# Moving the large GpSimd tensor operations of the layer ends to VectorE in a two-layer encoder

## The chip, the cores and the metric

The kernel runs on one core of a Trainium2 chip. The metric is the device time in microseconds (us) of one execution; the median of several executions is used. One execution was recorded by the hardware profiler, and all rows below are of that one. Five engines of the core run side by side, each with its own queue of instructions in a fixed order: TensorE (PE in the rows, its weight loads PEld), VectorE (DVE), ScalarE (ACT), GpSimd (POOL) and SyncE (SP, which here only starts DMA transfers).

## The reference

Two encoder layers on 512 tokens of width 1024. Each layer has a mixer (an mLSTM branch and a dilated attention branch) and a SwiGLU channel mixer of width 2816. Each of the two sub-layers ends in a scaled residual and a LayerNorm:

```
h = layer_norm(x)
for l in range(DEPTH):
    ...
    u = h * (1.0 + sc1) + sh1
    y = mixer(u, ...)
    h = layer_norm(DN_ALPHA * h + g1 * y, ln1_g[l], ln1_b[l])
    u = h * (1.0 + sc2) + sh2
    y = swiglu(u, w1[l], w3[l], w2[l])
    h = layer_norm(DN_ALPHA * h + g2 * y, ln2_g[l], ln2_b[l])
```

The shift, scale and gate vectors (sh, sc, g) are products of the conditioning vector with `w_ada`, plus a bias. All values are 32-bit floats.

## The kernel before

**Products.** Each float matrix product is done as three matmuls: both factors are split into a high part (a cast on ScalarE, line 87) and a low part (source minus high, a tensor_tensor on one engine, line 88), and high x high, high x low and low x high are summed (lines 91 to 93). The low part of nearly every weight tile is made on VectorE. `split` takes the engine as an argument; before the change GpSimd gets it for the early weights named below.

**Layer ends.** `out_norm` (line 408) is the end of a sub-layer. It is called four times; its name stands ahead of every tile: `o0` and `o1` are the mixer ends of layers 0 and 1, `f0` and `f1` the ends of the channel mixers. It multiplies the sub-layer's activations by the last weight (1024 output columns as two halves, y0 and y1; four blocks of 128 tokens, t = 0 to 3), adds the gated result to the residual (`gate`, `add`, lines 444 and 447), takes statistics (450, 352, 354; the power -1/2 is a tiny operation on GpSimd, line 355) and normalises (365). `to_u` then transposes the normalised block on TensorE (`turn`, line 381), applies the next scale and shift on ScalarE (`high`, lines 389 and 391) and makes the low part on VectorE (`low`, line 395).

**What is kept between sub-layers.** The kernel stores the normalised rows without LayerNorm's own g and b. The next layer end loads them (`loads`, line 426, tiles `f0x`, `o1x`, `f1x`) and applies g and b there: lines 430 and 431, one multiplication and one addition of 128x1024 for each token block, on GpSimd. That is done for four blocks in f0 and f1 and for two in o1; the other two blocks of o1 get it already in f0's `store` (lines 488 and 489), ahead of the store itself, which GpSimd's queue starts.

**Early weights.** While the last half of a layer end is running, the weights of the next product are made ready: `ahead` in the mixer ends splits the first two tiles of `w1` and `w3` (tiles `zw`; 2 layers x 4 tiles x 2 halves = 16 operations of 128x512 on line 88), and `ahead_next` in f0 splits the first query weights of layer 1 (`fw<-aqraw`, 8 operations of 128x512).

**Order.** Most of the program is put in order by the framework's scheduler, which places an instruction by the time it expects it to be ready: so the loads of f0 and f1 (lines 426 to 431) run far ahead, inside the channel mixer (`z` products of `w1` and `w3`, `sl` the activation, `L1337` the product with z3, `fl` its low part). The channel mixer's loop also carries background work: the `w_ada` products (`acc`, lines 281 and 283, one 128x512 operation for each of eight loaded tiles `aw`) and a transposition of the sum on TensorE (`adaps`, line 293). The second half of each layer end is written out by hand (`manual_schedule`): its order is the order of the code. In f0 and f1 TensorE goes through the last half in steps of two weight tiles (`pairs`) for blocks 2 and 3, and the steps of blocks 0 and 1 are dealt out between them by the tables `SD` and `SF`; the last six tiles are then done block by block (`columns`).

Of the kernel before, what the change touches and what calls it, by code (L numbers as in the profile page):

```python
# [14 lines left out]
ALU = mybir.AluOpType  # L15
# [5 lines left out]
KT = 8  # L21
# [44 lines left out]
def encoder(ctx: ExitStack, tc: tile.TileContext, a, depth):  # L66
    nc = tc.nc
    alpha = 4 ** 0.25
    V, S, G, Y = nc.vector, nc.scalar, nc.gpsimd, nc.sync
# [13 lines left out]
    def raw_tile(name):  # L83
        return wpool.tile([P, 2048], F32, tag="raw", name=name, bufs=RAW)

    def split(hi, lo, src, eng=None):
        S.copy(hi, src)  # L87
        (eng or V).tensor_tensor(lo, src, hi.bitcast(F32), op=ALU.subtract)  # L88
# [24 lines left out]
    def w_pair(name, off, k, n):  # L113

        return [wpool.tile([P, 1024 + WPAD], F32R, tag=t, name=name + t[1])[:, off:off + k * n]
                .rearrange("p (k n) -> p k n", n=n) for t in ("wh", "wl")]

    def w_feature(src, ktiles, name, own=None, count=2, eng=None):


        n = src.shape[1]
        cols = 2048 // ktiles
        srcv = src.rearrange("(k p) n -> p k n", p=P)
        for c0 in range(0, n, cols):
            cw = min(cols, n - c0)
            raw = raw_tile(name)
            rv = raw[:, :ktiles * cw].rearrange("p (k n) -> p k n", k=ktiles)
            Y.dma_start(rv, srcv[:, :, c0:c0 + cw])
            for j in range(cw // P):
                r = rv[:, :, j * P:(j + 1) * P]  # L130
                if own is not None and c0 // P + j < count:
                    yield split_own(r, ktiles, own, eng)
                    continue
                wh, wl = w_pair(name, 0, ktiles, P)
                split(wh, wl, r, G if name in POOL else V)
                yield [wh[:, k, :] for k in range(ktiles)], [wl[:, k, :] for k in range(ktiles)]

    def split_own(r, ktiles, own, eng):

        out = [], []  # L140
        for k in range(0, ktiles, 4):
            wh, wl = own(), own()
            split(wh[:], wl[:], r[:, k:k + 4, :], eng)
            for o, w in zip(out, (wh, wl)):
                o.extend(w[:, i, :] for i in range(4))
        return out

    def w_token(src, c0, cw, ktiles, name, own=None, own_k=(), early=False):

        srcv = src.rearrange("(k p) n -> p k n", p=P)  # L150
        per_raw = 2048 // cw
        per = 1024 // cw
        cuts = list(range(0, ktiles, per_raw)) + [ktiles]
        raws = []

        def load():
            i = len(raws)
            if i + 1 < len(cuts):
                k0, k1 = cuts[i], cuts[i + 1]
                raw = raw_tile(name)  # L160
                raws.append(raw[:, :(k1 - k0) * cw].rearrange("p (k n) -> p k n", n=cw))
                Y.dma_start(raws[i], srcv[:, k0:k1, c0:c0 + cw])

        if early:
            load()
        for i, (k0, k1) in enumerate(zip(cuts, cuts[1:])):
            load()
            rv = raws[i]
            for j in range(0, k1 - k0, per):
                m = min(per, k1 - k0 - j)  # L170
                if k0 + j in own_k:
                    for h in range(m):
                        wh, wl = own(), own()
                        split(wh[:], wl[:], rv[:, j + h, :])
                        yield wh[:], wl[:]
                else:
                    wh, wl = w_pair(name, SH if cw == 256 else 0, per, cw)
                    split(wh[:, :m], wl[:, :m], rv[:, j:j + m, :])
                    for h in range(m):
                        yield wh[:, h, :], wl[:, h, :]  # L180
# [227 lines left out]
    def out_norm(act, ktiles, w, l, which, prev, todo, own, final, aff, u, hin, hout, keep, name, ahead, after, fslot=None):  # L408

        with ExitStack() as st:  # L410
            lp = pool(st, name + "L", side="right")
            xs = [lp.tile([P, D], F32, name=f"{name}x{t}") for t in range(NT)]
            rows = {}

            def row(key, src, q=Y):
                rows[key] = lp.tile([P, D], F32, tag="row" + key, name=name + key)
                q.dma_start(rows[key][:], src.partition_broadcast(P))

            def loads():
                row("g", adarow[l][which][0])  # L420
                if prev is not None:
                    row("s", prev[0])
                    row("b", prev[1])
                for t in range(NT):
                    x = xs[t]
                    Y.dma_start(x[:], hin[t * P:(t + 1) * P, :])
                    if prev is None:
                        V.tensor_scalar(x[:], x[:], mu0[t][:, 0:1], mu0[t][:, 3:4], op0=ALU.subtract, op1=ALU.mult)
                    elif t in todo:
                        G.tensor_tensor(x[:], x[:], rows["s"][:], op=ALU.mult)  # L430
                        G.tensor_tensor(x[:], x[:], rows["b"][:], op=ALU.add)
                if own is not None:
                    row("s", own[0], G)
                    row("b", own[1], G)
# [50 lines left out]

            def store(t):
                if own is not None and t < 2:
                    G.tensor_tensor(xs[t][:], xs[t][:], rows["s"][:], op=ALU.mult)
                    G.tensor_tensor(xs[t][:], xs[t][:], rows["b"][:], op=ALU.add)
                (G if own is not None and t < 2 else S).dma_start(hout[t * P:(t + 1) * P, :], xs[t][:])  # L490

            def side_steps(y01):

                todo = []
                for t in range(2):
                    steps = consume_steps(y01[t], t, 1) + norm_steps(t)
                    if not final:
                        turn, high, low = to_u(lp, xs[t], t, aff, u, name + "n")
                        steps.extend([turn, step(high, 0), step(low, 0), step(high, 1), step(low, 1), step(store, t)])
                    todo.extend(zip((SF if final else SD)[t], steps))  # L500
                if not final:
                    for i, ats in enumerate((AQL, AQS)):
                        todo.extend((at, step(ahead, i, n)) for n, at in enumerate(ats))
                return todo
# [16 lines left out]
            if keep:  # L521
# [6 lines left out]
                w1 = w_token(w, T, T, ktiles, name + "v", oh, range(4, ktiles), True)  # L528
                for k in range(4):
                    wk_ = next(w0)  # L530
                    for t in range(NT):
                        part(acc[t], t, k, *wk_)
                    if k == 1:
                        loads()
# [13 lines left out]
            else:  # L548
                for k, wk_ in enumerate(w_token(w, 0, T, ktiles, name + "w")):
                    for t in range(NT):  # L550
                        part(acc[t], t, k, *wk_)
                    if k == 1:
                        loads()
# [19 lines left out]
                w1 = w_token(w, T, T, ktiles - 2, name + "v", fslot, range(2 * heads, ktiles - 6))  # L573
# [70 lines left out]
    with ExitStack() as st:  # L644
        lp = pool(st, "L0", side="right")
        xs = [lp.tile([P, D], F32, name=f"x0{t}") for t in range(NT)]
# [74 lines left out]
        with tc.manual_schedule(engines=ENG):  # L721
            for f in range(KT):
                wh, wl, _ = wq
# [11 lines left out]
    for l in range(depth):  # L735
# [554 lines left out]
        def hgw():  # L1290
            return PW.tile([P, 4, P], F32R, tag="hgw", name="zw", bufs=16)

        w1 = w_feature(a["w1"][l], KT, "w1", hgw, 2, G)
        w3 = w_feature(a["w3"][l], KT, "w3", hgw, 2, G)
        quad, zs, third = [], [], []

        def ahead():
# [22 lines left out]
        for i in range(FT):  # L1320
# [12 lines left out]
            t = F.tile([P, T], F32, tag="sl", name="sl", bufs=1)  # L1333
# [14 lines left out]
        first_w, first, first_k, aq_raw = [], [], {}, []  # L1348

        def fslot():  # L1350
            return F.tile([P, T], F32R, tag="f", name="fw", bufs=2 * FT)

        def ahead_next(part, n):

            if part == 0:
                c0 = COL_A + 512 * (n // 2)
                raw = F.tile([P, T], F32, tag="f", name="aqraw", bufs=2 * FT)[:].rearrange("p (k n) -> p k n", k=4)
                Y.dma_start(raw, a["w_in"][l + 1][512 * (n % 2):512 * (n % 2) + 512, c0:c0 + P]
                            .rearrange("(k p) n -> p k n", p=P))
                aq_raw.append(raw)  # L1360
            else:
                wh, wl = (fslot()[:].rearrange("p (k n) -> p k n", k=4) for _ in range(2))
                split(wh, wl, aq_raw[n], G)
                if n % 2 == 0:
                    first_w.append(([], []))
                for o, w in zip(first_w[-1], (wh, wl)):
                    o.extend(w[:, i, :] for i in range(4))
# [61 lines left out]
```

## Time and profile before

| | us |
|---|---|
| median of 3 runs | 2280.37 (2280.28 to 2283.35) |
| profiled execution, its own time | 2288.52 |
| span of the profiled execution | 2286.7 |
| TensorE busy | 2201.6 (96%) |
| VectorE busy | 1315.9 (58%) |
| ScalarE busy | 884.0 (39%) |
| GpSimd busy | 321.6 (14%) |
| mean granted TensorE clock | 0.985 |

The span is the time from the first to the last instruction of the profiled execution; its own time is 1.8 us longer, and 8.15 us above the median of the runs without a profile. Busy times are of all instructions of an engine, and overlap between engines. The granted clock is the share of TensorE's full speed (2.4 GHz) that the chip allowed; 0.5 is 1.2 GHz.

### The profile page before, as it was taken

Reading aid. Unit: us, or ns where it says so; the run is one execution under the profiler, and the core shown is the slowest. Engines: PE = TensorE matmul, PEld = TensorE weight load, DVE = VectorE, ACT = ScalarE, POOL = GpSimd, SP = SyncE. Lnnn points to the kernel's source line nnn. Section 1 sums busy time; section 2 is a strip of 40 time slices with the busy share of each in tenths; the row PEclk is TensorE's granted clock in tenths of the full one; section 3 lists DMA queues with packets and bytes.
Section 4 is the critical chain, followed back from the end, with each engine's and each line's share of the span. In section 5 each row is a group of like instructions: output and inputs, shape, how many; then the busy total and the mean of one; then the engine's idle time right before and its main releaser. Section 6 shows DMA issues by size and latency. Waiting matters only on the chain.

```text
span 2286.7 us, 30972 instructions
## 1 busy us (share of the span) xinstructions
PE 2201.6 (96%) x12353; PEld 1836.4 (80%) x12353; DVE 1315.9 (58%) x2242; ACT 884.0 (39%) x1465; POOL 321.6 (14%) x318
## 2 busy tenths in 40 slices
PE   6999999999999999999989999999999999999998
PEld 5878877878888878788878788788888879788886
DVE  8655458778554766564654544577764454633346
ACT  3544345544333522222354443455543324223222
POOL 4100013222000240000040000233300022200001
PEclk8999999999999999999999999999999999999999
DMA  8523322232343466554543223112212344423334
GB/s 239 186 83 107 101 66 97 74 111 80 111 157 113 155 206 205 189 193 167 189 152 98 61 92 107 56 62 69 74 56 92 111 157 157 152 83 102 100 112 157
DMA packets 244064, 278.79 MB, mean 122 GB/s; under 512 B 10280, under 2 KB 191184, under 8 KB 243920
## 3 DMA queue, kind: packets, MB, share of 16 engines
q1 hardware_dynamic: 238848, 258.97, 35.1%
q0 software_dynamic: 3584, 12.58, 1.6%
q10 hardware_dynamic: 1488, 5.26, 0.6%
q8 instruction: 97, 1.59, 0.3%
q14 instruction: 47, 0.39, 0.1%
HBM read 264.18 MB, written 12.60 MB: 121 GB/s over the span
## 4 chain that ended last, share of the span: by engine, by line
PE 75%; DVE 14%; ACT 3%; issue 3%; DMA 3%; POOL 2%; POOLq 0%; DVEq 0%; ACTq 0%; SPq 0%
PE z L93 6%; PE z L92 6%; PE z L91 6%; DVE cy L1081 4%; DMA aw<-in_w_ada 2%; PE aq L91 2%; PE ak L91 2%; PE f1y L92 2%; PE av L91 2%; PE f1y L91 2%; PE f1y L93 2%; PE av L93 2%; PE av L92 2%; PE aq L93 2%; PE aq L92 2%
## 5 line engine op out<-in xcount | busy, mean ns | idle before, releaser
L283 DVE SCALAR_TENSOR_TENSOR acc<-aw,cact,acc 128x512 f32<-128x512 f32 x140 | 118.3, 845 | 49.8 <-DMA aw<-in_w_ada 47.6
L1081 DVE SCALAR_TENSOR_TENSOR cy<-zp,vcols,cy 128x512 f32<-128x512 f32 x128 | 115.6, 903 | 10.4 <-ACT cy L1079 8.5
L87 ACT CAST w3h<-w 128x1024 fp32r<-128x1024 f32 x40 | 42.1, 1053 | 157.3 <-PE z L92 153.2
L88 POOL TENSOR_TENSOR wqkl<-wqk,wqkh 128x1024 fp32r<-128x1024 f32 x32 | 78.0, 2438 | 161.4 <-ACT wqkh L87 159.5
L978 ACT ACTIVATE xs<-xs,sm 128x512 f32<-128x512 f32 x64 | 46.2, 723 | 133.3 <-DVE sm L977 129.6
L87 ACT CAST w1h<-w 128x1024 fp32r<-128x1024 f32 x40 | 42.0, 1050 | 139.9 <-PE z L92 134.9
L88 DVE TENSOR_TENSOR w1l<-w,w1h 128x1024 fp32r<-128x1024 f32 x40 | 49.4, 1234 | 77.3 <-ACT w1h L87 77.3
L1337 DVE TENSOR_TENSOR sl<-sl,z 128x512 f32<-128x512 f32 x44 | 30.2, 687 | 104.9 <-PE z L93 101.2
L976 DVE CUSTOM_DVE_ANT_0 xs<-sc,bias 128x512 f32<-128x512 f32 x64 | 43.9, 691 | 74.7 <-PE sc L970 63.7
L91 PE MATMUL z<-um0h,w3h 128*128 128x512 f32 x160 | 64.2, 401 | 4.0 <-DVE sl L1337 4.0
L91 PE MATMUL z<-um1h,w3h 128*128 128x512 f32 x160 | 63.5, 397 | 1.8 <-DVE sl L1337 1.8
L93 PE MATMUL z<-um1h,w3l 128*128 128x512 f32 x160 | 63.6, 398 | 1.0 <-DVE w3l L88 1.0
L93 PE MATMUL z<-um0h,w3l 128*128 128x512 f32 x160 | 63.9, 400 | 0.5 <-DVE w3l L88 0.5
L92 PE MATMUL z<-um0l,w3h 128*128 128x512 f32 x160 | 63.8, 399 | 0.0
L92 PE MATMUL z<-um1l,w3h 128*128 128x512 f32 x160 | 63.2, 395 | 0.0
L91 PE MATMUL z<-um0h,w1h 128*128 128x512 f32 x160 | 63.1, 394 | 0.0
L93 PE MATMUL z<-um0h,w1l 128*128 128x512 f32 x160 | 62.7, 392 | 0.0
L92 PE MATMUL z<-um0l,w1h 128*128 128x512 f32 x160 | 62.5, 391 | 0.0
L91 PE MATMUL z<-um1h,w1h 128*128 128x512 f32 x160 | 62.4, 390 | 0.0
L93 PE MATMUL z<-um1h,w1l 128*128 128x512 f32 x160 | 62.3, 390 | 0.0
L92 PE MATMUL z<-um1l,w1h 128*128 128x512 f32 x160 | 62.2, 389 | 0.0
L935 POOL DMA_DIRECT2D vrow<-nat x16 | 11.8, 736 | 345.0 <-ACT nat L928 344.9
(544 smaller groups left out, 7268.0 us busy)
## 6 DMA issues: line engine op xcount, KB each, us to landing
w<-in_w SPq DMA_DIRECT2D x44, 1024.0 KB
aw<-in_w_ada SPq DMA_DIRECT2D x160, 256.0 KB
wqk<-in_w_in SPq DMA_DIRECT2D x16, 1024.0 KB
wav<-in_w_in SPq DMA_DIRECT2D x12, 1024.0 KB
wak<-in_w_in SPq DMA_DIRECT2D x20, 512.0 KB
f0v<-in_w SPq DMA_DIRECT2D x10, 1024.0 KB
f1v<-in_w SPq DMA_DIRECT2D x10, 1024.0 KB
waq<-in_w_in SPq DMA_DIRECT2D x18, 512.0 KB
```

The costliest lines, as they stand in the source:

```text
L87: S.copy(hi, src)
L88: (eng or V).tensor_tensor(lo, src, hi.bitcast(F32), op=ALU.subtract)
L91: mm(out, lh, rh, start=first, stop=False)
L92: mm(out, lh, rl, start=False, stop=False)
L93: mm(out, ll, rh, start=False, stop=last)
L283: V.scalar_tensor_tensor(acc[:], raws[k][:], c, acc[:], op0=ALU.mult, op1=ALU.add)
L935: G.dma_start(rows[i0 * P:(i0 + 2) * P, :].rearrange("(i p) c -> p i c", p=P), nat[:])
L976: V.tensor_tensor_reduce(x[:], sc[:], bias_tile(ti), 1.0, -3e38, ALU.add, ALU.max, sm[:, 0:1])
L978: S.activation(x[:], x[:], AF.Exp, bias=sm[:, 1:2], scale=ch, accum_out=sm[:, 2:3])
L1081: V.scalar_tensor_tensor(y[:], zp[:, j:j + T], vec["conv"](j, n), y[:], op0=ALU.mult, op1=ALU.add)
L1337: V.tensor_tensor(t[:], t[:], p3[:], op=ALU.mult)
```

## The change

Lines 430, 431, 488 and 489 and the low parts of the early weights (line 88 as called by way of lines 1293, 1294 and 1363) go from GpSimd to VectorE. Nothing else is edited; the two stores of line 490 stay in GpSimd's queue.

```diff
                     elif t in todo:
-                        G.tensor_tensor(x[:], x[:], rows["s"][:], op=ALU.mult)
-                        G.tensor_tensor(x[:], x[:], rows["b"][:], op=ALU.add)
+                        V.tensor_tensor(x[:], x[:], rows["s"][:], op=ALU.mult)
+                        V.tensor_tensor(x[:], x[:], rows["b"][:], op=ALU.add)
...
             def store(t):
                 if own is not None and t < 2:
-                    G.tensor_tensor(xs[t][:], xs[t][:], rows["s"][:], op=ALU.mult)
-                    G.tensor_tensor(xs[t][:], xs[t][:], rows["b"][:], op=ALU.add)
+                    V.tensor_tensor(xs[t][:], xs[t][:], rows["s"][:], op=ALU.mult)
+                    V.tensor_tensor(xs[t][:], xs[t][:], rows["b"][:], op=ALU.add)
...
-        w1 = w_feature(a["w1"][l], KT, "w1", hgw, 2, G)
-        w3 = w_feature(a["w3"][l], KT, "w3", hgw, 2, G)
+        w1 = w_feature(a["w1"][l], KT, "w1", hgw, 2)
+        w3 = w_feature(a["w3"][l], KT, "w3", hgw, 2)
...
-                split(wh, wl, aq_raw[n], G)
+                split(wh, wl, aq_raw[n])
```

VectorE's queue gets 36 more rows of the kind shown below (a row may stand for several equal instructions); the queues of TensorE and ScalarE keep their order. GpSimd keeps the powers, the memsets, its DMAs and the splits of the mixer.

On VectorE, in the channel mixer of layer 0 (the places of the loads of f0; the four numbers 9233 to 9236 are the four token blocks), the scheduler puts the eight operations between those of two steps of the mixer's loop:

```order
 L88 TENSOR_TENSOR w1l<-w_7426,w1h 128x1024
+L430 TENSOR_TENSOR f0x_9233<-f0x_9233,f0s 128x1024
+L431 TENSOR_TENSOR f0x_9233<-f0x_9233,f0b 128x1024
+L430 TENSOR_TENSOR f0x_9234<-f0x_9234,f0s 128x1024
 L1337 TENSOR_TENSOR sl<-sl,z_7524 128x512
+L431 TENSOR_TENSOR f0x_9234<-f0x_9234,f0b 128x1024
+L88 TENSOR_TENSOR fl<-sl,fh 128x512
 L88 TENSOR_TENSOR w3l<-w_7432,w3h 128x1024
-L88 TENSOR_TENSOR fl<-sl,fh 128x512
+L430 TENSOR_TENSOR f0x_9235<-f0x_9235,f0s 128x1024
+L430 TENSOR_TENSOR f0x_9236<-f0x_9236,f0s 128x1024
+L431 TENSOR_TENSOR f0x_9235<-f0x_9235,f0b 128x1024
```

Seven of the eight new operations now stand in VectorE's queue among `L1337`, `fl` and `w3l` of one step of the loop; the eighth (`L431` of block 3) follows nine rows later, just ahead of the next `L1337`.

On VectorE, in the part of f0 written by hand (`f0vl` is the low part of a pair of the last weight, `uf0l` that of a block's next input, `fw<-f0v` and the last two `f0vl` the tiles of the `columns`):

```order
 L395 TENSOR_TENSOR uf0l<-f0nut,uf0h 128x4x128
+L488 TENSOR_TENSOR f0x_9233<-f0x_9233,f0s 128x1024
+L489 TENSOR_TENSOR f0x_9233<-f0x_9233,f0b 128x1024
 L88 TENSOR_TENSOR f0vl<-f0v,f0vh 128x1024
 L395 TENSOR_TENSOR uf0l<-f0nut,uf0h 128x4x128
 L88 TENSOR_TENSOR f0vl<-f0v,f0vh 128x1024
 L395 TENSOR_TENSOR uf0l<-f0nut,uf0h 128x4x128
+L488 TENSOR_TENSOR f0x_9234<-f0x_9234,f0s 128x1024
+L489 TENSOR_TENSOR f0x_9234<-f0x_9234,f0b 128x1024
 L88 TENSOR_TENSOR fw<-f0v,fw 128x512 x2
+L88 TENSOR_TENSOR fw<-aqraw,fw 128x512 x2
 L88 TENSOR_TENSOR f0vl<-f0v,f0vh 128x1024 x2
```

The scale and shift of blocks 0 and 1 now stand ahead of low parts of weights that TensorE reads next, and so does the first pair of early weights.

On VectorE, in o1 (blocks 2 and 3 are `o1x_16344` and `o1x_16345`):

```order
 L444 TENSOR_TENSOR o1tmp<-o1y_16351,o1g 128x512
+L430 TENSOR_TENSOR o1x_16344<-o1x_16344,o1s 128x1024
 L447 SCALAR_TENSOR_TENSOR o1x_16343<-o1x_16343,o1tmp 128x512
+L431 TENSOR_TENSOR o1x_16344<-o1x_16344,o1b 128x1024
+L430 TENSOR_TENSOR o1x_16345<-o1x_16345,o1s 128x1024
 L450 BN_STATS o1st_16347<-o1x_16343 128x6
+L431 TENSOR_TENSOR o1x_16345<-o1x_16345,o1b 128x1024
 L444 TENSOR_TENSOR o1tmp<-o1y_16352,o1g 128x512
```

The four operations now stand between the gating of block 1 and that of block 2; further down, four `zw` operations stand between the statistics of block 3 (first half) and the gating of block 0 (second half).

## Rows read from the trace of the kernel before

**Rows 1.** The page's first part: busy time, share of the span, instructions
```profile
PE 2201.6 (96%) x12353; PEld 1836.4 (80%) x12353; DVE 1315.9 (58%) x2242; ACT 884.0 (39%) x1465; POOL 321.6 (14%) x318
```
**Rows 2.** Busy time by stretch; columns PE, PEld, DVE, ACT, POOL, PEclk, DMA, GB/s
```profile
755.00:785.00 30.00, 29.48 (x165) 25.32 (x164) 24.46 (x36) 16.80 (x39) 13.85 (x12) 1.00 0.45 156
830.00:845.00 15.00, 10.53 (x37) 7.72 (x35) 11.24 (x13) 2.59 (x4) 5.33 (x4) 0.77 0.58 190
1138.00:1157.00 19.00, 13.59 (x59) 10.41 (x59) 16.29 (x11) 9.31 (x19) 12.89 (x7) 0.91 0.75 241
1157.00:1182.00 25.00, 21.70 (x123) 18.10 (x122) 17.41 (x20) 15.07 (x31) 14.95 (x13) 1.00 0.27 89
1876.00:1891.00 15.00, 11.40 (x34) 7.63 (x34) 14.36 (x14) 3.13 (x6) 11.09 (x7) 0.77 0.28 90
1957.00:1971.00 14.00, 11.21 (x39) 8.39 (x38) 9.85 (x11) 2.69 (x4) 3.03 (x3) 0.76 0.51 156
940.00:953.00 13.00, 10.81 (x43) 8.54 (x42) 7.26 (x12) 3.21 (x4) 0.00 (x0) 0.87 0.53 182
```
**Rows 3.** Instructions grouped by line, GpSimd: count | busy us, mean ns | idle before
```profile
L88 POOL TENSOR_TENSOR fw<-aqraw,fw 128x512 fp32r<-128x512 f32 x8 | 12.8, 1626 | 9.6 <-ACT fw L87 9.6
...
L430 POOL TENSOR_TENSOR f0x<-f0x,f0s 128x1024 f32<-128x1024 f32 x4 | 11.2, 2800 | 29.3 <-DMA f0x<-hspill 29.3
```
**Rows 4.** Timeline of VectorE where GpSimd is idle: start, duration, instruction
```profile
790.52 1.23 DVE L88 TENSOR_TENSOR w1l<-w,w1h 128x1024 fp32r<-128x1024 f32 x1 [0.26 <-ACT w1h L87]
791.66 1.22 DVE L88 TENSOR_TENSOR w3l<-w,w3h 128x1024 fp32r<-128x1024 f32 x1
...
1856.93 2.49 DVE L88 TENSOR_TENSOR o1o<-o1w,o1o 128x512 fp32r<-128x512 f32 x4
```
**Rows 5.** Timelines of GpSimd, VectorE and TensorE at the loads of f0
```profile
811.56 2.40 POOL L430 TENSOR_TENSOR f0x<-f0x,f0s 128x1024 f32<-128x1024 f32 x1 [29.32 <-DMA f0x<-hspill]
...
822.80 2.35 DVE L296 TENSOR_TENSOR scc<-scc,vcols 128x4 f32<-128x4 f32 x1
...
834.78 0.67 DVE L1337 TENSOR_TENSOR sl<-sl,z 128x512 f32<-128x512 f32 x1
...
847.82 0.16 DVE L296 TENSOR_TENSOR shc<-shc,vcols 128x4 f32<-128x4 f32 x1
...
835.60 0.76 PE L91 MATMUL z<-um0h,w3h 128*128 128x512 f32 x1 [3.96 <-DVE sl L1337]
```
**Rows 6.** Timelines of ScalarE, VectorE and TensorE at the end of f0
```profile
1136.45 1.05 ACT L87 CAST f0vh<-f0v 128x1024 fp32r<-128x1024 f32 x1 [1.67 <-PE f0y L93]
1139.17 1.06 ACT L87 CAST f0vh<-f0v 128x1024 fp32r<-128x1024 f32 x1 [1.67 <-PE f0y L93]
...
1140.13 2.91 DVE L365 TENSOR_SCALAR f0x<-f0x,f0nmv,f0nrs 128x1024 f32<-128x1024 f32 x1 [0.45 <-POOL f0nrs L355]
1142.96 3.38 DVE L88 TENSOR_TENSOR f0vl<-f0v,f0vh 128x1024 fp32r<-128x1024 f32 x1
...
1143.10 1.09 PE L381 MATMUL f0ntp<-ident,f0x 128*128 128x128 f32 x8 [0.33 <-DVE f0x L365]
...
1180.50 1.09 PE L381 MATMUL f0ntp<-ident,f0x 128*128 128x128 f32 x8
```
**Rows 7.** Timelines of VectorE and TensorE in o1
```profile
1870.12 0.69 DVE L444 TENSOR_TENSOR o1tmp<-o1y,o1g 128x512 f32<-128x512 f32 x1 [0.57 <-PE o1y L93]
...
1878.58 7.20 DVE L88 TENSOR_TENSOR o1o<-o1v,o1o 128x512 fp32r<-128x512 f32 x4
...
1880.76 0.50 PE L92 MATMUL o1y<-o1o,mh 128*128 128x512 f32 x1 [2.30 <-DVE o1o L88]
...
1893.77 1.03 PE L381 MATMUL o1ntp<-ident,o1x 128*128 128x128 f32 x8
```
**Rows 8.** VectorE's timeline at the loads of f1; TensorE's waits from 1918 us on
```profile
1960.19 0.68 DVE L1337 TENSOR_TENSOR sl<-sl,z 128x512 f32<-128x512 f32 x1
...
PE z L91 <- DVE sl L1337: 1.8, 1, 1.8
```

## The prediction

> **What bounds the kernel now.** I read the page's busy times first: TensorE works 96% of the span, every other engine at most 58% [rows 1]. So a change on VectorE and GpSimd can pay only where TensorE stands still or runs at a lower clock. Next I read TensorE's waits and, around them, the stretches of the four layer ends [rows 2]. The time lost in a stretch is its length less the PE busy time, plus (1 - PEclk) times its length: 0.5 us in o0 (755 to 785), 4.5 + 3.45 = 7.9 at the loads of f0 (830 to 845), 5.4 + 1.7 + 3.3 = 10.4 at the end of f0 (1138 to 1182), 3.6 + 3.45 = 7.05 in o1 (1876 to 1891), 2.8 + 3.35 = 6.15 at the loads of f1 (1957 to 1971): 32.0 us in all. That is the most the change can give back in these places.
>
> Then I read the timelines there, to see what is late. TensorE always waits for VectorE (for `sl`, `f0vl`, `o1o`), and VectorE is late because its instructions grow while GpSimd works on large tiles. `L296`, 128x4, takes 2.35 us while line 430 or 431 runs, and 0.16 us later on [rows 5]; `f0vl` takes 3.38 us [rows 6] where its like takes 1.22 [rows 4]; four `o1o` take 7.20 us [rows 7] against 2.49 [rows 4]. The reader should see that such an instruction lasts about as long as what is left of a GpSimd operation of 2.4 to 2.8 us [rows 3, 5], plus its own time. VectorE is blocked there, not overloaded.
>
> The SBUF — State Buffer page of the Trainium skill (Who interferes with whom) says that the two engines share a port pair which one of them holds for its whole instruction; the long 128x4 operation of this trace agrees. By that rule alone, all 32.0 us would return; this is the full recovery below.
>
> **The change, step by step.** Removed from GpSimd: 24 operations of 128x1024 at about 2.8 us and 24 of 128x512 at about 1.6 [rows 3]. Added to VectorE: the same 48. The trace has no `L430` on VectorE; the nearest rows are subtractions with the same two SBUF inputs and shape, which follow each other after 1.14 us (790.52 to 791.66) and take 2.49 / 4 = 0.62 us at 128x512 [rows 4]. GpSimd's own 2.8 us is the upper bound, and 0.62 the lower (as if size cost nothing); I take 1.14, since engine, shape and operands are the same. Added: 24 x 1.14 + 24 x 0.62 = 42 us, against 2286.7 - 1315.9 us in which VectorE is idle. What counts is where they stand, so I re-timed each place: the new order of VectorE's queue, undisturbed durations, TensorE at 0.227 us per 512-column matmul (two ScalarE casts of neighbouring weight pairs, 12 matmuls apart, are 2.72 us apart [rows 6]).
>
> *o0.* Four `zw` (2.5 us) come ahead of block 0's gating, but the VectorE work around them is no longer blocked. Block 0 is normalised at 765.0, when TensorE is ready to transpose it. Gain 0.5 us.
>
> *Loads of f0.* VectorE reaches `L430` when the first block lands (811.56, the end of GpSimd's wait [rows 5]). Eight operations add 9.1 us up to the second `L1337`, with `w1l`, `w3l` and the `acc` work between them; I get `L1337` done at about 828.5 instead of 835.45. TensorE stood ready for it at 835.60 - 3.96 = 831.64 [rows 5]: 3 us to spare. The low parts of w1 and w3 then come about 0.7 us before they are read, and the background sum, paced by its loads, just in time. Of 7.9 I take 7.5.
>
> *End of f0.* From 1140.13 on [rows 6]: `L365` of block 1 ends at 1140.9, the next `f0vl` at 1142.0, so TensorE transposes block 1 at 1142.6, not 1143.10, and does not wait behind it. The store's two operations (2.3 us) then stand before the next low parts. They delay the `f0vl` of the pair after next to 1150.1, where TensorE wants it at 1149.1: a wait of 1.0. Block 1's pair delays `fw` and, with two early weights, the `f0vl` behind: waits of 0.7 and 1.5. Four early weights (2.5 us) delay block 3's gating, and its transposition by 0.5. Without waits TensorE has 0.85 (transposition) + 4 x 2.72 (pairs) + 2 x 4.08 (last six tiles of blocks 2 and 3) + 0.85 + 42 x 0.12 (256-column products) = 25.8 us from 1142.6 to the transposition of block 3, which would be at 1168.4; now it is at 1180.50 [rows 6]. With the 3.8 us of new waits it comes at 1172.2. Gain 8.3 us.
>
> The Perfetto Trace Analysis page (Optimizing Scalar/DVE Operations) of the Trainium skill advises giving work to GpSimd when VectorE is saturated, and adds that this might not help because of the shared port. It speaks against the change, and is the third rival below.
>
> *o1.* After the gating at 1870.12 [rows 7] VectorE has two blocks to scale and shift (4.6 us) and then the usual steps, and starts the four `o1o` at 1878.5, as now (1878.58), but ends them at 1881.0, not 1885.8. TensorE, ready for the first at 1880.76 - 2.30 = 1878.46, waits 0.8. After that four `zw` (2.5 us) stand in front of block 0's gating, and its normalised rows come at 1889.5. TensorE would transpose them at 1887.15 (1878.1 + 2.72 for the rest of block 0 + 5.44 for block 1 + 0.9), so it waits 2.35 us, on a wait that does not exist now. The transposition is at 1889.5 instead of 1893.77 [rows 7]: 4.2 us. In the stretch 940 to 953 TensorE stood for about 2.2 us and the granted clock was 0.87, which cost 0.13 x 13 = 1.7 us [rows 2]; I charge 1.7 here too. Gain 2.5 us.
>
> *Loads of f1.* The same eight operations, and less background work. `L1337` is done at about 1955 instead of 1960.87 [rows 8]; TensorE needs it by 1959. The wait of 1.8 us [rows 8], the one for `w3l` and the clock's 3.35 go. Of 6.15 I take 6.0.
>
> *Not on the path:* the last half of f1 has none of the moved work. The four stores and row loads in GpSimd's queue start earlier or at the same time and are read much later. The powers on GpSimd keep their place behind short operations. What is hidden behind TensorE now stays so as long as VectorE is less than 2.5 us late in f0's loads; past that each us costs one.
>
> Sum: 0.5 + 7.5 + 8.3 + 2.5 + 6.0 = 24.8 us. The profiled execution took 2288.52 us (span 2286.7 and 1.8 around it), so a profile should show about 2263.7. The runs without a profile have a median of 2280.37; carrying the same gain over gives 2255.6 us, 1.1% faster. This kernel's measurement can tell 0.2% (4.6 us).
>
> **The rivals.**
>
> *Full recovery.* The new waits (3.8 in f0, 0.8 and 2.35 in o1 and the clock's 1.7 there) don't arise, because undisturbed VectorE work ahead of them leaves more room than I count. For it: I took every start from a queue that was disturbed before. Against: the new operations stand in front of what TensorE waits for, by the code's own order. Gain 32, time 2248.4.
>
> *The waits move to VectorE.* The low parts of weights in the two ends written by hand come late after all, and each new wait of 1.5 us or more draws a lower clock, as in 940 to 953. The end of f0 and o1 then give back 0 and -2 instead of 8.3 and 2.5; the loads still gain 13.5 and o0 0.5. Gain 12, time 2268. For it: VectorE is busy 16.29 of 19 us in 1138 to 1157 [rows 2]. Against: much of that is blocked time.
>
> *VectorE is the bound: slower.* If in these places the 42 us of added work all fell on the path, the change would cost 42 - 32 = 10 us: 2290. It decides where less than 10 of the 42 us are hidden in time in which VectorE idles now. Against it: it idles 2.7 + 7.6 us in 1138 to 1182 alone [rows 2], for 9.5 us added there, and the loads of f0 have the margin worked out above.
>
> *VectorE waits for the residual loads.* GpSimd could stand 29.3 us for `f0x` and harm nobody [rows 5]; VectorE can't. If the blocks land late, everything behind `L430` is late, and beyond 2.5 us so is TensorE. A landing 8 us later in f0 and f1 alike would eat 11 of the 13.5 us, and the time would be 2267. Against: the first block's landing releases at 811.56, just when VectorE gets there, and SyncE's queue is the same up to that place.
>
> *Nothing changes.* Waits behind the layer ends, for `aw` loads, could take up what TensorE gains. Then 2280. Against: those loads are started as VectorE frees their buffers, so they move with it.
>
> **How the numbers follow.** My case (gain 18 to 28) 0.55; full recovery 0.17; the waits move to VectorE 0.14; late loads 0.05; nothing changes 0.05; VectorE the bound 0.04. Faster: the first four, less a little for late loads, 0.91; same 0.05; slower 0.04. The range leaves out the last two, part of full recovery and the worst of moved waits: 2246 to 2268 (at 1.14 us per operation; the lower bound of that price would remove the new waits, which is full recovery, the upper one would make the loads of f0 late by more than 10 us and is as good as VectorE the bound).
>
> **What the next profile would show.** Right: `L296` and the other small VectorE operations at 0.2 us throughout; `L430` on VectorE at 1.2 us; no wait of TensorE for `sl` near 831 and 1959; PEclk of 1.0 there; a wait for `f0vl` or `fw` of 1 to 2 us at three places near the end of f0, and one for `o1x` of about 2 us at the first transposition of o1. Wrong: `L430` at 2 us or more; VectorE's idle time ended by `f0x` loads; `L1337` after 831; the time of f0's end unchanged with `f0vl` still the wait.

## The result and the profile after

The changed kernel takes 2258.61 us (median of 4 runs, 2257.21 to 2260.34), the kernel before in the same measurement 2280.32 (4 runs). The ratio is 0.9903, 95% interval 0.9889 to 0.9917: 1.0% faster, 21.7 us by the medians. The forecast was 2255.6 in a range of 2246 to 2268. The profiled execution took 2259.71 us, its span is 2257.9.

The page's busy line, which answers to [rows 1]:

```profile
PE 2189.0 (97%) x12353; PEld 1831.3 (81%) x12353; DVE 1307.3 (58%) x2290; ACT 883.7 (39%) x1465; POOL 220.0 (10%) x270
```

VectorE has 48 instructions more, and is busy 8.6 us less. The added work is worth about 42 us at the prices of the forecast, which held (below), so some 50 us of its earlier busy time were time in which it was held.

Busy time by stretch; each stretch holds about the work that the one in [rows 2] held, in the order o0, loads of f0, the stretch behind them, end of f0 (two), o1, loads of f1. Columns: length, PE, PEld, DVE, ACT, POOL, PEclk, DMA share, GB/s.

```profile
753.00:783.00 30.00, 30.00 (x169) 25.85 (x168) 25.33 (x45) 17.03 (x40) 2.19 (x4) 1.00 0.45 158
825.00:840.00 15.00, 15.00 (x70) 12.43 (x69) 11.24 (x18) 3.81 (x5) 0.53 (x1) 1.00 0.77 242
928.50:941.50 13.00, 12.08 (x56) 9.80 (x55) 9.37 (x16) 3.19 (x4) 0.00 (x0) 1.00 0.65 218
1127.00:1146.00 19.00, 16.92 (x77) 13.06 (x75) 16.04 (x18) 16.68 (x33) 1.35 (x3) 1.00 0.75 241
1146.00:1161.00 15.00, 13.82 (x86) 12.08 (x87) 12.67 (x22) 6.29 (x15) 2.73 (x5) 1.00 0.33 104
1859.00:1875.00 16.00, 13.98 (x57) 11.38 (x58) 14.27 (x26) 6.70 (x16) 1.09 (x2) 0.89 0.43 141
1932.00:1946.00 14.00, 14.00 (x66) 11.60 (x65) 9.39 (x14) 3.59 (x5) 0.00 (x0) 1.00 0.53 177
```

Lost time is again the length less PE, plus (1 - PEclk) times the length. At both loads nothing is left of 7.9 and 6.15 us: TensorE is busy all the time, at the full clock. At the end of f0, 2.1 + 1.2 = 3.3 us are left of 10.4. In o1, 2.0 + 1.8 = 3.8 are left, and 0.8 just ahead of the stretch: 4.6 of 7.05. Those are new waits.

TensorE's waits in the whole trace, those in the layer ends (total, times, longest); no wait for `sl` is among them:

```profile
PE f0y L92 <- DVE f0vl L88: 2.2, 2, 1.3
PE o1ntp L381 <- DVE o1x L365: 2.0, 1, 2.0
...
PE o1y L92 <- DVE o1o L88: 0.8, 1, 0.8
PE f0ntp L381 <- DVE f0x L365: 0.6, 1, 0.6
...
PE f0y L92 <- DVE fw L88: 0.3, 1, 0.3
```

Timelines of VectorE and TensorE, at the places of [rows 5 to 8]:

```profile
809.06 1.22 DVE L430 TENSOR_TENSOR f0x<-f0x,f0s 128x1024 f32<-128x1024 f32 x1
...
821.09 0.15 DVE L296 TENSOR_TENSOR scc<-scc,vcols 128x4 f32<-128x4 f32 x1
...
824.91 0.68 DVE L1337 TENSOR_TENSOR sl<-sl,z 128x512 f32<-128x512 f32 x1
...
1131.03 1.23 DVE L88 TENSOR_TENSOR f0vl<-f0v,f0vh 128x1024 fp32r<-128x1024 f32 x1 [0.88 <-ACT f0vh L87]
...
1858.26 2.48 DVE L88 TENSOR_TENSOR o1o<-o1v,o1o 128x512 fp32r<-128x512 f32 x4
...
1868.41 0.81 DVE L365 TENSOR_SCALAR o1x<-o1x,o1nmv,o1nrs 128x1024 f32<-128x1024 f32 x1 [0.73 <-POOL o1nrs L355]
...
1160.22 1.09 PE L381 MATMUL f0ntp<-ident,f0x 128*128 128x128 f32 x8 [0.62 <-DVE f0x L365]
...
1869.28 1.70 PE L381 MATMUL o1ntp<-ident,o1x 128*128 128x128 f32 x8 [2.02 <-DVE o1x L365]
```

The 128x4 `L296` takes 0.15 us instead of 2.35, four `o1o` 2.48 instead of 7.20, and `L430` on VectorE 1.22. The last row has the new wait of o1, and its eight products, which take 1.09 us in f0, take 1.70: they run at the lower level of the clock (1.2 of 2.4 GHz; the granted clock is 0.54 from 1869.3 to 1873 us) after a wait of 2 us.

The two profiled executions are 2288.52 - 2259.71 = 28.8 us apart, the medians 21.7. Before's profiled execution lay above all its other runs (2275.9 to 2283.35), so part of the 28.8 is that execution's own.

### The profile page after: what moved, and what is told of

Its sections match the earlier page's. It is cut to its first block, busy times and chain, and to the rows that moved or that the text cites. A ratio compares the mean times of both kernels' runs of the same rounds, so it can differ in the third digit from the quotient of the medians.

```text
span 2257.9 us, 30948 instructions
## 1 busy us (share of the span) xinstructions
PE 2189.0 (97%) x12353; PEld 1831.3 (81%) x12353; DVE 1307.3 (58%) x2290; ACT 883.7 (39%) x1465; POOL 220.0 (10%) x270
## 3 DMA queue, kind: packets, MB, share of 16 engines
q8 instruction: 97, 1.59, 0.3%
## 4 chain that ended last, share of the span: by engine, by line
PE 76%; DVE 13%; DMA 4%; ACT 3%; issue 2%; POOL 1%; POOLq 0%; DVEq 0%; SPq 0%; ACTq 0%
PE z L92 6%; PE z L91 6%; PE z L93 6%; DVE cy L1081 5%; DMA aw<-in_w_ada 2%; PE aq L91 2%; PE ak L91 2%; PE aq L93 2%; PE aq L92 2%; PE ak L93 2%; PE ak L92 2%; PE f1y L92 2%; PE f1y L93 2%; PE f1y L91 2%; DVE acc L677 2%
## 5 line engine op out<-in xcount | busy, mean ns | idle before, releaser
L283 DVE SCALAR_TENSOR_TENSOR acc<-aw,cact,acc 128x512 f32<-128x512 f32 x140 | 110.1, 786 | 45.9 <-DMA aw<-in_w_ada 43.8
L1081 DVE SCALAR_TENSOR_TENSOR cy<-zp,vcols,cy 128x512 f32<-128x512 f32 x128 | 115.6, 903 | 10.4 <-ACT cy L1079 8.5
L1337 DVE TENSOR_TENSOR sl<-sl,z 128x512 f32<-128x512 f32 x44 | 30.2, 687 | 100.1 <-PE z L93 96.4
L87 ACT CAST wqkh<-wqk 128x1024 fp32r<-128x1024 f32 x32 | 33.6, 1049 | 47.8 <-PE o L92 37.4
```

Source lines behind the costliest of these rows:

```text
L283: V.scalar_tensor_tensor(acc[:], raws[k][:], c, acc[:], op0=ALU.mult, op1=ALU.add)
L1081: V.scalar_tensor_tensor(y[:], zp[:, j:j + T], vec["conv"](j, n), y[:], op0=ALU.mult, op1=ALU.add)
L1337: V.tensor_tensor(t[:], t[:], p3[:], op=ALU.mult)
```

## The experiments

Medians in us. Each row was measured beside the kernel before on the same chip, and the ratio is to that. It is not the quotient of the two medians, and the two can differ: the loads alone are 14.2 us faster by the medians and 11 us (7 to 15) by the ratio. In the three parts of the change and the two runs with idle work, as in the change itself, TensorE and ScalarE have the same instructions in the same order as the kernel before.

| kernel | median | before there | ratio, 95% interval |
|---|---|---|---|
| loads alone | 2267.99 | 2282.17 | 0.9952, 0.9936 to 0.9969 |
| store alone | 2278.93 | 2282.17 | 0.9992, 0.9981 to 1.0003 |
| early weights alone | 2278.74 | 2282.17 | 0.9986, 0.9977 to 0.9996 |
| changed, idle GpSimd reads | 2271.70 | 2282.17 | 0.9958, 0.9943 to 0.9973 |
| changed kernel again | 2257.50 | 2281.69 | 0.9899, 0.9884 to 0.9914 |
| changed, idle GpSimd writes | 2257.59 | 2281.69 | 0.9896, 0.9881 to 0.9911 |
| changed, later order | 2254.33 | 2281.69 | 0.9880, 0.9863 to 0.9897 |
| changed, wqk on VectorE | 2246.95 | 2281.69 | 0.9853, 0.9834 to 0.9872 |
| the last two together | 2241.56 | 2280.61 | 0.9832, 0.9818 to 0.9847 |
| and q, k low parts | 2229.83 | 2280.61 | 0.9777, 0.9763 to 0.9790 |
| and the program's start | 2224.91 | 2283.01 | 0.9754, 0.9740 to 0.9768 |

**One part of the change at a time.** First the loads alone (lines 430 and 431):

```
-                        G.tensor_tensor(x[:], x[:], rows["s"][:], op=ALU.mult)
-                        G.tensor_tensor(x[:], x[:], rows["b"][:], op=ALU.add)
+                        V.tensor_tensor(x[:], x[:], rows["s"][:], op=ALU.mult)
+                        V.tensor_tensor(x[:], x[:], rows["b"][:], op=ALU.add)
```

> Only lines 430 and 431 (scale and shift at the loads of f0, o1 and f1) go to VectorE; the store and the early weights stay on GpSimd. Theory (VectorE was blocked by GpSimd's large operations): the waits of TensorE for sl near 831 and 1959 go, 7.4 + 6.2 us as in the changed kernel, o1 gains 2 to 5 us because its residual blocks no longer block o1o, and the end of f0 keeps its waits of 7 us for f0vl. About 16 to 19 us below the kernel before: 2262 to 2265 us. Rival (each part of the change gives about the same share of 22 us, by instruction count 20 of 48): about 9 us, 2271 us.

It gains 14.2 us by the medians and 11 by the ratio, less than expected; it is the largest part. The time alone does not exclude the rival's 9 us, but the places do: no wait for `sl` is left, and the end of f0 keeps 5.7 us of waits for `f0vl` (7.3 before). In o1 the reason that I gave fails. Timelines of VectorE and GpSimd:

```profile
1860.74 6.74 DVE L88 TENSOR_TENSOR o1o<-o1v,o1o 128x512 fp32r<-128x512 f32 x4
...
1860.60 6.33 POOL L88 TENSOR_TENSOR zw<-w,zw 128x512 fp32r<-128x512 f32 x4 [124.97 <-ACT zw L87]
```

The early weights `zw` hold the four `o1o` nearly as long as before (7.20 us [rows 7]); in the kernel before, too, `zw` ran beside most of them (1880.12 to 1886.92 us), behind the residual's last operation. TensorE still waits 3.9 us for them (3.6 before); what o1 gains is the clock, 1.00 instead of 0.77. Then the store alone (the same edit in lines 488 and 489):

> Only lines 488 and 489 (scale and shift ahead of the store of f0's blocks 0 and 1, 4 operations) go to VectorE. Theory: the two long waits for f0vl between 1143 and 1153 and the lower clock behind them go, one new wait of about 1 us for f0vl comes, and the waits while fw is split stay. 4 to 6 us below the kernel before: about 2275 us; all other stages as before. Rival by instruction count (4 of 48): 2 us, not to be told from no change.

It can't be told from no change (3.2 us by the medians): that is the rival's number, not mine. TensorE's waits for `f0vl` do fall from 7.3 to 1.1 us, as expected. The reason for the rest stands in its timelines of VectorE, GpSimd and TensorE:

```profile
1148.77 6.45 DVE L88 TENSOR_TENSOR fw<-f0v,fw 128x512 fp32r<-128x512 f32 x2
...
1149.15 0.54 POOL L490 DMA_DIRECT2D hspill<-f0x  x1 [5.80 <-DVE f0x L489]
1149.70 4.97 POOL L88 TENSOR_TENSOR fw<-aqraw,fw 128x512 fp32r<-128x512 f32 x4
...
1155.28 0.80 PE L92 MATMUL f0y<-fw,fh 128*128 128x512 f32 x1 [4.81 <-DVE fw L88]
```

GpSimd now waits for VectorE's `L489` before it can store block 1, and its early weights stand behind that in its queue. Their casts are done by then, so four come in a row, where the kernel before had two and two. One VectorE subtraction of 128x512 is held through all four: 6.45 us for two that take 1.29 in the changed kernel. TensorE stands 4.81 us for it. What one part gives back, the part that was left on GpSimd takes. Third, the early weights alone (`zw` and `fw`):

```
-        w1 = w_feature(a["w1"][l], KT, "w1", hgw, 2, G)
-        w3 = w_feature(a["w3"][l], KT, "w3", hgw, 2, G)
+        w1 = w_feature(a["w1"][l], KT, "w1", hgw, 2)
+        w3 = w_feature(a["w3"][l], KT, "w3", hgw, 2)
...
-                split(wh, wl, aq_raw[n], G)
+                split(wh, wl, aq_raw[n])
```

> Only the low parts of early weights (zw, fw from aqraw; 24 operations of 128x512) go to VectorE. Theory: the end of f0 gains the 2 to 4 us of waits after 1160, o0 gains 0.5 us, o1 gains little or loses up to 2 us, since four zw stand in front of block 0's gating while o1o is still blocked by the residual's operations; the loads of f0 and f1 keep their waits. 1 to 5 us below the kernel before: about 2277 us. Rival by instruction count (24 of 48): 11 us, 2269 us.

It gains 3.4 us by the medians, as expected. By the medians the three parts sum to 20.8 us, and the whole is worth 21.7 (24.2 where it was measured again); by the ratios they sum to 16, and the whole is worth 22 to 23. So these runs don't show whether the parts add up or whether the whole is worth more than they are, which the traces of the loads alone and of the store alone would suggest.

**Does GpSimd's work harm without anybody using it?** The changed kernel, with eight products and sums of 128x1024 on GpSimd at the loads of f1, whose result nobody reads:

```
+ final and [G.tensor_tensor(sel[:].rearrange("p j m -> p (j m)"), rows["s"][:], rows["b"][:], op=o)
+            for o in (ALU.mult, ALU.add)]
```

> The changed kernel, and in the loads of f1 GpSimd is given eight operations of 128x1024 of the same kind and at the same place as before the change, but of which nobody uses the result: they read the LayerNorm rows and write a constant tile that is not used any more. Theory (the operations hurt by blocking VectorE, whoever uses their result): VectorE's small instructions near 1915 to 1935 grow to 1.5 to 3 us again, the wait of TensorE for sl and the lower clock come back, and more, as VectorE now has its own eight operations there too: 6 to 12 us above the changed kernel, 2264 to 2271 us. Rival (what was slow was to wait for GpSimd's results): no wait, and the time of the changed kernel, 2258.6 us.

It is 2271.70 where the changed kernel has 2257.5 to 2258.6: 13 to 14 us are lost, a little more than expected. The rival falls: no data leads from these operations to anything. Timelines of GpSimd, VectorE and TensorE:

```profile
1910.06 24.76 POOL L430 TENSOR_TENSOR sel<-f1s,f1b 128x1024 fp32r<-128x1024 f32 x8 [24.06 <-DMA f1b<-in_ln_b]
...
1915.94 6.75 DVE L430 TENSOR_TENSOR f1x<-f1x,f1s 128x1024 f32<-128x1024 f32 x2
1922.62 6.67 DVE L431 TENSOR_TENSOR f1x<-f1x,f1b 128x1024 f32<-128x1024 f32 x2
...
1930.03 0.77 PE L91 MATMUL z<-um1h,w3h 128*128 128x512 f32 x1 [5.77 <-DVE sl L1337]
```

VectorE's operations take 3.4 us each instead of 1.22, in turns with GpSimd's of 24.76 / 8 = 3.1, and TensorE has its wait for `sl` back, and the lower clock (0.85 granted from 1905 to 1940 us). The same place again, with GpSimd work that only writes:

```
+ final and [G.tensor_tensor(sel[:, 0, 0:8], rows["s"][:, 0:8], rows["b"][:, 0:8], op=ALU.mult)]
+         + [G.memset(sel[:].rearrange("p j m -> p (j m)").bitcast(F32), 0.0) for _ in range(5)]
```

> The changed kernel with idle GpSimd work at the loads of f1 again, but now work that only writes: four times a 128x8 product (the wait for the loaded rows) and five fills of a 128x1024 tile with zeros, instead of the eight 128x1024 products and sums that read two tiles and cost 13 us. Theory that VectorE is held by GpSimd's reading of tiles in SBUF: little is lost, 2257 to 2262. Rival, that any large GpSimd instruction in SBUF holds VectorE for its length: the fills are shorter, VectorE is late at the same place, 2263 to 2272.

Nothing is lost (2257.59 against 2257.50), though GpSimd is nearly as busy as with the reads (22.2 us of 1905 to 1940, against 24.8). Timelines of GpSimd and VectorE:

```profile
1913.15 5.01 POOL L430 MEMSET sel<- 128x1024 f32 x5
...
1911.81 2.36 DVE L430 TENSOR_TENSOR f1x<-f1x,f1s 128x1024 f32<-128x1024 f32 x2
1914.09 2.35 DVE L431 TENSOR_TENSOR f1x<-f1x,f1b 128x1024 f32<-128x1024 f32 x2
1916.36 0.67 DVE L1337 TENSOR_TENSOR sl<-sl,z 128x512 f32<-128x512 f32 x1
```

Four VectorE operations beside the fills take 1.18 us each. So it is not GpSimd's being busy that holds VectorE. What the fills lack is the reading of tiles; they are also another kind of instruction, which these two runs alone don't separate. The SBUF — State Buffer page of the Trainium skill (Who interferes with whom) names the reading: a VectorE instruction with two SBUF inputs contends with a GpSimd instruction that reads SBUF, and not with one that only writes. The two runs agree, with 3.4 against 1.18 us.

**The waits that are left.** In the changed kernel two `ahead()` calls stand ahead of block 0's gating; here they stand behind its normalisation. And f0's stores of blocks 0 and 1 go behind the gating of block 3:

```
-SD = ((0, 0, 0.5, 1, 1.5, 3, 3.5, 4, 4.5, 5, 5), (1, 1.5, 2, 2, 2.5, 4, 5.5, 6, 6.5, 7, 7))
+SD = ((0, 0, 0.5, 1, 1.5, 3, 3.5, 4, 4.5, 5, 10), (1, 1.5, 2, 2, 2.5, 4, 5.5, 6, 6.5, 7, 10))
...
-                ahead()
-                ahead()
...
+                    if t == 0:
+                        ahead()
```

> The changed kernel with the waits that the change left taken away by order alone: in the mixer ends the four zw low parts that stand ahead of block 0's gating go behind its normalisation, and in f0 the scale, shift and store of blocks 0 and 1 go behind the consumption of block 3. My theory, that TensorE's waits for o1x (2.0 us and 1.7 of low clock behind it) and for f0vl at the end of f0 (2.2) come from these instructions standing ahead in VectorE's queue: 3 to 6 us below the changed kernel, 2253 to 2256. Rival, that the instructions moved are late elsewhere (the zw of block 1's turn, or the hidden store ahead of f0's last normalisation): no gain, 2257 to 2262.

3.2 us less by the medians, with intervals that overlap, so the size is uncertain. The place is not: in its waits (as above) the two rows read

```profile
PE f0y L92 <- DVE f0vl L88: 0.7, 1, 0.7
...
PE o1ntp L381 <- DVE o1x L365: 0.2, 1, 0.2
```

and the lower clock behind the first transposition of o1 is gone, too: its granted clock is 1.00 in the stretch that holds it. The instructions stood in the way by their order alone.

**GpSimd elsewhere.** The changed kernel leaves 32 low parts of `wqk` in the mixers on GpSimd. One line moves them:

```
-POOL = ("wqk",)
+POOL = ()
```

> The changed kernel with the last large GpSimd operations of the mixer, the 32 low parts of wqk (128x1024), on VectorE too. If large GpSimd operations harm wherever they stand, 3 to 8 us below the changed kernel (2250 to 2256). If they cost only where TensorE waits for VectorE in the same microseconds, and the mixer's are covered by other work, within 3 us of it, or slower where the 32 x 1.2 us stand ahead of what TensorE wants: 2256 to 2270.

10.6 us less, more than I expected of either. Timelines of GpSimd and VectorE in the mixer of the changed kernel (the profile of the run called changed kernel again):

```profile
1503.20 2.39 POOL L88 TENSOR_TENSOR wqkl<-wqk,wqkh 128x1024 fp32r<-128x1024 f32 x1
...
1503.38 2.23 DVE L1189 TENSOR_TENSOR dn<-dn,gcols 128x1 f32<-128x1 f32 x1
```

A product of 128x1, 0.15 us by itself, lasts as long as GpSimd's subtraction; with the low parts on VectorE the longest of its 64 takes 0.16 us. But TensorE waits for nothing near this place, so this is not the gain yet. TensorE's waits with the `wqk` low parts on VectorE (in the changed kernel the row for `zp` is 10.7, 8 times):

```profile
PE num L91 <- DVE vl L1106: 5.2, 6, 2.5
...
PE mv L91 <- ACT zp L1077: 0.6, 1, 0.6
```

The waits for ScalarE's `zp` are what went, about as much as the gain. Timelines of VectorE, ScalarE and TensorE at the longest of them, in the same profile of the changed kernel:

```profile
1467.67 3.09 DVE L1081 SCALAR_TENSOR_TENSOR cy<-zp,vcols,cy 128x512 f32<-128x512 f32 x4
...
1470.86 0.63 ACT L1082 ACTIVATE zp<-cy 128x512 f32<-128x512 f32 x1 [2.37 <-DVE cy L1081]
...
1472.02 0.38 PE L91 MATMUL mv<-wvh,uf0h 128*128 128x256 f32 x1 [2.62 <-ACT zp L1077]
```

ScalarE stands behind four VectorE products in a row, so the engine named in the table of waits is not the first cause. But GpSimd does not hold them: they take 0.77 us each, their median is 0.75, and GpSimd has no large operation from 1465.7 to 1472.6 us. And this edit changes more than the engine. The framework's scheduler puts 41 of ScalarE's 1465 instructions elsewhere in its queue, and some of TensorE's; the four products then stand as two and two, with a low part between them. So the run shows that held time goes and that the waits for `zp` go, but not that the one causes the other: how much of the 10.6 us is held time and how much the new order stays open. The two improvements together:

> Both improvements in one kernel: the later order of the low parts and the store in the layer ends (3.2 us alone) and the wqk low parts of the mixer on VectorE (10.6 us alone). They stand in different stages, so theory: they add, 2243 to 2246, the fastest kernel so far. Rival, that waits behind them take up part of the gain: 2246 to 2250.

16 us below the changed kernel, 14 were the sum; by the ratios it is 15 and 15, so they add up. Then the 32 low parts of q and k too:

```
-GQ = (0, 1)
+GQ = ()
```

> The kernel with both improvements and, besides, the 32 low parts of q and k (128x512, about 1.3 us each on GpSimd) on VectorE. If every large read by GpSimd costs, 2 to 4 us less again (2240 to 2244). If what is left of them lies where VectorE has room, and 32 x 0.7 us of added work on VectorE lie ahead of what TensorE wants, no gain or a loss: 2244 to 2252.

11.7 us less: three times what I expected at best. The mixer of layer 0, by stretch, ahead of this step and behind it:

```profile
320.00:560.00 240.00, 231.17 (x1381) 198.46 (x1380) 188.22 (x396) 119.92 (x220) 32.33 (x68) 0.99 0.29 91
```

```profile
320.00:560.00 240.00, 238.21 (x1424) 204.01 (x1423) 193.73 (x435) 128.39 (x242) 10.13 (x52) 1.00 0.30 95
```

TensorE stands still for 1.8 us of 240 instead of 8.8. The scheduler has changed the order here too (28 of ScalarE's instructions stand elsewhere), so this gain is not shown to be held time alone either. Last, the program's start:

```
-            G.tensor_tensor(u[1][:, f, :], ut[:], u[0][:, f, :].bitcast(F32), op=ALU.subtract)
+            V.tensor_tensor(u[1][:, f, :], ut[:], u[0][:, f, :].bitcast(F32), op=ALU.subtract)
...
-        split(wq[0][:], wq[1][:], wq[2], G)
+        split(wq[0][:], wq[1][:], wq[2])
...
-                    split(wq[0][:], wq[1][:], wq[2], G)
+                    split(wq[0][:], wq[1][:], wq[2])
```

> The kernel before this one and the last large GpSimd operations, at the very start of the program, on VectorE: eight wql (128x768, 2.0 us each on GpSimd) and eight u0l (128x512, 1.6 us). If the rule of the layer ends and the mixer holds here too, 2 to 5 us less than 2229.8. Rival: here VectorE itself is what TensorE waits for (acc, 11 us), so 8 x 0.9 + 8 x 0.7 = 13 us of added VectorE work stand ahead of it and at most the blocked time returns: same or up to 6 us slower, 2229 to 2236.

4.9 us less (by the ratios, whose intervals overlap a little, 5), so the rival falls. TensorE's waits for the sum at the start (`acc`, line 678) go from 11.0 to 6.9 us, and the order hardly changes (3 of ScalarE's instructions). Its page:

```profile
PE 2176.5 (98%) x12353; PEld 1822.4 (82%) x12353; DVE 1301.5 (59%) x2370; ACT 884.6 (40%) x1465; POOL 65.7 (3%) x190
```

VectorE now has all 128 large operations that GpSimd had in the kernel before, and is busy 14 us less than with none of them [rows 1].

## Why the prediction was right

The likeliest case came, with its mechanism; 2258.61 is 3.0 above the forecast. Taking lost time before less lost time after, from the windows:

- *o0*: 0.5 forecast, 0.5 found.
- *Loads of f0*: 7.5 forecast, 7.9 found. `L1337` was done at 825.6, and TensorE reached the product that needs it at 829.1: 3.5 us to spare where I had 3, and nothing came late behind it. (The execution of the changed kernel is 2.5 us ahead when it comes to this place, so most of the 3 us by which 825.6 lies ahead of my 828.5 is no margin.)
- *End of f0*: 8.3 forecast, 7.1 found. All four new waits came, at like sizes (`f0vl` 0.9 and 1.3, not 1.0 and 1.5; `fw` 0.3, not 0.7; `f0ntp` 0.6, not 0.5): 3.1 against 3.7 us, which my sum rounded to 3.8. The term is still about 1 us too large. From block 1's transposition (1129.74 in the changed kernel) to block 3's (1160.22) it is 30.5 - 3.1 = 27.4 us without the waits, not 25.8. The products themselves follow each other as I counted, after 0.227 and 0.12 us; what I left out stands around the waits. Each costs TensorE 0.2 to 0.3 us more than its row (from product to product the 1.29 us for `f0vl` are 1.55), and another 0.3 us stand ahead of block 2's transposition.
- *o1*: 2.5 forecast; 7.05 - 4.6 = 2.4 found. The wait for `o1o` was 0.8, as forecast, the one on block 0's turn 2.0, not 2.35, and the lower clock behind it 1.8, not 1.7.
- *Loads of f1*: 6.0 forecast, 6.15 found.

The sum is 24.1 against 24.8. The profiled execution was 4 us below its forecast of 2263.7, since 28.8 - 24.1 = 4.7 us of the difference lie outside these places. Of them, 3.0 lie in the stretch behind f0's loads (940 to 953 before): 2.2 + 1.7 = 3.9 us were lost there, now 0.9. They are not the change's. The same stretch in the store alone, and in the early weights alone:

```profile
934.00:947.00 13.00, 12.17 (x57) 9.86 (x56) 9.39 (x16) 3.19 (x4) 0.00 (x0) 1.00 0.72 237
```

```profile
934.00:947.00 13.00, 12.96 (x60) 10.47 (x60) 10.19 (x16) 3.18 (x4) 0.00 (x0) 1.00 0.76 251
```

Both leave the loads of f0 on GpSimd, and the first changes nothing that stands ahead of this stretch; they lose 0.8 us and nothing there. So this loss belongs to the one execution of the kernel before that was profiled, the slowest of all its runs on record. The remaining 1.7 us lie elsewhere in the program, where the two kernels do the same.

The last step, that a profile's gain carries over to the median, held within the noise: the medians fell by 21.7 us, with an interval of 19 to 25 that holds 24.8, and by 24.2 where the changed kernel was measured again.

The rivals. *Full recovery* did not come: TensorE still waits at six places, four in f0 and two in o1, and the run with the later order shows that the longest could go. *The waits move to VectorE*: they moved only as far as the sum has them. Nor is this rival's price of the clock in the rows: in the kernel before, TensorE's products still follow each other after 0.23 us behind its waits of 1.97 us (1146.40) and 1.59 us (1165.50); behind the 2.02 us of o1 in the changed kernel it is 0.43. *VectorE the bound*: `L430` costs 1.22 us there, near the 1.14 that I took. The Perfetto Trace Analysis page of the Trainium skill (Optimizing Scalar/DVE Operations) says that giving some of a saturated VectorE's work to GpSimd may make sense, with the warning that it might not help. Here VectorE is busy 58%, and the other way paid: each step that gave VectorE more work made the kernel faster, down to 2224.91 us, but for the store alone, which can't be told from no change. *Late residual loads*: VectorE waited 0.5 us once for `f0x`. *Nothing changes*: the `aw` loads moved with VectorE; between 780 and 960 us SyncE's longest wait for the sum `acc` fell from 5.8 to 2.0 us.

## What to carry to other kernels

Look for small VectorE instructions that last as long as what GpSimd has under way: they price the engines' collision, and the work moved may cost less than the time that it frees. The engine named in the table of waits need not be the one to blame: in the mixer it was ScalarE, which waited for VectorE. Move all of such work that meets in one place; one half alone can gain little, because the other half still holds what it held, or stands closer together. And where a scheduler sets the order, compare the queues of all engines before a gain is put down to the engine that was changed.

## What was not expected

- One VectorE subtraction was held through four GpSimd operations in a row (4.97 us), not through the rest of one. At the loads of f1 the two engines took turns instead, 3.4 and 3.1 us.
- With the loads alone the four `o1o` still took 6.74 us: the early weights `zw` hold them more than the residual's operations do.
- VectorE with 128 operations more was busy 14 us less.
- The wait of 2.19 us and the lower clock at 940 to 953 us, from which the forecast took its price of the clock, were that one execution's own; the price itself (1.7 us) was met in o1 (1.8).
